# One encoder layer on one core: an earlier scaling, weights in pieces, and a down projection begun with A12

## The chip, the cores and the metric

The kernel runs on one core of a Trainium2 chip. The metric is device time in microseconds: how long one execution takes. A core has five engines that run side by side, each through its own list of instructions in order: TensorE (PE: matmuls and transposes; PEld is its weight load), VectorE (DVE), ScalarE (ACT), GpSimd (POOL) and SyncE (SP, which here issues nearly all DMAs). An instruction that has to wait holds back everything behind it on its engine.

## The reference

The layer is computed for 1024 sample rows and 256 prompt rows, 1024 wide, all in fp32:

```python
h = rmsnorm(x, g_mix);  z = h @ w_in                      # 1024 x 5120
o_a = banded attention, 8 heads with sinks, 2 kv heads    # window 128
o_b = mixture of three dilated groups of 4 heads, weighted by softmax of their log-sums
merged = sigmoid(gate_a) * (o_a @ w_branch_a) + sigmoid(gate_b) * (o_b @ w_branch_b)
x = x + merged @ w_out
h = rmsnorm(x, g_mlp)
x = x + square(relu(h @ w_up)) @ w_down                   # 4096 wide inside
y = rmsnorm(x, g_final)
```

Prompt and sample are two separate sequences with the same weights.

## The kernel before

**Products.** Every fp32 operand is split into a rounded part `hi` (on ACT) and the rest `lo` (on DVE), and a product is three matmuls (hi hi, hi lo, lo hi). For the sample's rows the large products use Strassen's scheme with Winograd's seven products: operands are cut into 2 x 2 blocks, and seven products of sums of blocks (`A11, A12, S2, S3, S1, A22, S4`) give the four blocks of the result. `seven()` is one such product, twelve matmuls with 512 columns; `six()` on L347 holds its matmul, so most matmuls of the profile have that line. The prompt's rows are multiplied plainly by `prompt()`.

**Stages, by the time of the profile.** (1) 0 to 120 us: rows are loaded, normed (`square`: ACT's sum of squares and root; `scale`: DVE's reciprocal and scaling), transposed on PE (`turn`) and split; meanwhile `values` makes the value columns of `z`. (2) 120 to 541 us: the other columns of `z` in pairs of 128 (`pair`, 16 of them); in the last seven, the mixed stage (`late` is true there), the dilated attention is interleaved step by step (`tick`, `beside`). (3) up to about 690 us the banded attention, then gates, merge and output product; this part is ordered by a planner, all others by hand in program order. (4) 890 to 1294 us: the up product in 16 rounds (`up(j)`), whose results `u`, one tile for each of the seven left operands of the next product, are stored in DRAM (`scr_u`). (5) 1294 us to the end: the down product (`Down`).

**Right operands.** `right_pair` is a generator. It loads two tiles of 128 columns (`raw`), forms the sums of blocks `ta`, `tb` and splits four tiles (`raw[0]`, `ta`, `tb`, `raw[1]`); each `yield` is a place where the caller goes on with its own work, and `next` or `steps_of(gen, n)` takes one or n steps. In `pair` the tiles for the next pair are prepared during the present one. The split of a tile is `split_steps`: ACT on L312, DVE on L314; in `Down` and elsewhere `split`: ACT L185, DVE L186.

**Buffers.** Tiles come from pools by kind, and a tile's first writer waits until the buffer is free: `slot` (33 buffers of 4 KB per partition), `wslot` (10 buffers), `stage` (one buffer per name during `up`), the pool `l4` during `Down`. The 28 + 4 buffers of split left operands fill nearly all of `slot` through `up` and come free as the last round ends with each.

**The up rounds.** `up(j)` computes its seven products, the two prompt products, the squared relu of each block and four sums on POOL (L1945 to L1948), then SP stores seven tiles of u. `hooks` is a generator whose steps are taken between products; in the last round it is `Down.begin`, which prepares the first jobs of down. `relu2_sum` (DVE L1873, L1874) finishes a block; `c1`, `c2`, `c7` are ACT's copies of a bank that PE goes on adding to.

**The down product.** `JOBS` is the order of 28 jobs (n, g): n is one of the seven products, g one of four groups of 1024 inner rows. A job is five row tiles t of twelve matmuls. Two neighbouring jobs (g even, g odd) add up in the same five PSUM banks; after the odd one DVE adds each bank to the running sums `v` (L1852) that began as the residual rows from `scr_x`. While job s runs, `ahead(s)` emits the loads and POOL's block differences (`combine`, L1698) for job s + 2 and the splits of the right and left sides for job s + 1: its first step after t = 0, the three left splits after t = 1 to 3. In the last two products of the last groups, and for two more, ACT squares each finished tile for the final norm (`square`, L1806), and POOL multiplies it with the final gain (L1809).

Of the kernel before, what the change touches and what calls it, by code (L numbers as in the profile page):

```python
# [15 lines left out]
P = 128  # L16
# [81 lines left out]
def encoder_kernel(  # L98
# [271 lines left out]
    def right_pair(cols, out, make=wslot, vector=False):  # L370

        raw = [make("raw", (P, KC, P)) for _ in range(2)]
        for i in range(2):
            nc.sync.dma_start(raw[i], cols[i])
        yield

        def part(src, shape):  # L380
            out.append((wslot("whi", shape, F32R), wslot("wlo", shape, F32R)))
            yield from split_steps(*out[-1], src)

        b11, b21, b12, b22 = raw[0][:, :4], raw[0][:, 4:], raw[1][:, :4], raw[1][:, 4:]
        if vector:
# [283 lines left out]
    with ExitStack() as pre:  # L669
# [174 lines left out]
        next(turns[0], None)  # L844
        pss = [bank("mm", "v") for _ in range(2)]
# [5 lines left out]
        square(3)  # L851
        next(turns[1], None)
        scale(3)
# [54 lines left out]
    if True:  # L908
# [104 lines left out]
        def pair(b, parts, cols, nxt, hooks, beside, late):  # L1013
# [6 lines left out]
            nb = right_pair([w_in3[:, :, c : c + P] for c in nxt], np_, wslot, late) if nxt else iter(())  # L1020
# [6 lines left out]
            def behind():  # L1027
                beside()
                if not late:
                    steps_of(b, 2)  # L1030

# [12 lines left out]
            one.direct(NS, NP, pa)  # L1044
            beside()
            seven(x, S2, parts[1], 0, False, False, beside)
# [3 lines left out]
            if late:  # L1050
                next(nb, None)
            z = bank("mm", "z")
            seven(z, S3, parts[1], 1, last=False, mid=beside)
# [3 lines left out]
            beside()  # L1057
            next(hooks, None)
            seven(x, S1, parts[2], 0, False, False, beside)
            two.sum(512, 512, x, c7)  # L1060
            beside()
            if not late:
                steps_of(nb, 3)
# [593 lines left out]
    JOBS = [(n, 2 * p + i) for p in range(NG // 2) for n in range(7) for i in range(2)]  # L1657

    class Down:
        def __init__(self):  # L1660
            self.blocks, self.sums, self.raw, self.rights, self.lefts = {}, {}, {}, {}, {}
            self.t, self.tags, self.late, self.banks, self.rs = {}, 0, None, {}, {}
# [4 lines left out]
        def block(self, g, k, h, make=wslot, queue=None):  # L1667

            b = self.blocks[g, k, h] = [make("raw", (P, 2, 512)) for _ in range(2)]
            for i in range(2):  # L1670
                j = 4 * g + 2 * i
                (queue or nc.sync).dma_start(b[i], w_down4[:, j : j + 2, k, 512 * h : 512 * h + 512])

        def loads(self, n, g):
            if n == 1:
                self.block(g, 1, 1, slot)
            elif n == 4:
                self.block(g, 1, 0, slot)
            elif n == 5 and g < NG - 2:
                self.block(g + 2, 0, 0)  # L1680
                self.block(g + 2, 0, 1)
# [71 lines left out]
        def begin(self):  # L1753

            self.block(0, 0, 0, wslot, nc.scalar)
            self.block(0, 0, 1, slot, nc.scalar)
            self.fetch(*JOBS[0])
            yield
            self.combine(*JOBS[0])
            yield  # L1760
            yield
            self.block(1, 0, 0)
            self.block(1, 0, 1)
            yield
            self.right(*JOBS[0], slot)
            self.combine(*JOBS[1])
# [3 lines left out]
            yield  # L1770
            self.fetch(*JOBS[1])
# [3 lines left out]
        def ahead(self, s):  # L1775
# [6 lines left out]
            if s in (0, 2, 4):  # L1782
                self.residual((C22, C11, C21)[s // 2])
            if s == 0:
                self.residual(C12)
# [42 lines left out]
        def go(self):  # L1828
            with tc.tile_pool(name="down", bufs=1) as self.late:
                for s, (n, g) in enumerate(JOBS):  # L1830
# [6 lines left out]
                    for t in range(5):  # L1837
# [3 lines left out]
                        next(side, None)  # L1841
                        if g % 2 == 0:
                            continue
# [9 lines left out]
                        if g == NG - 1 and n in (3, 4):  # L1853
                            self.square((C22, C12)[n - 3], t)
# [7 lines left out]
    with ExitStack() as pre:  # L1862
# [23 lines left out]
        begun = {}  # L1886

        def up(j, b, parts, hooks):
# [7 lines left out]
            u = [stage(f"u{i}", TH) for i in range(7)]  # L1896
            u11, u12, u22, u21 = u[A11], u[A12], u[A22], u[S3]
# [6 lines left out]
            next(hooks, None)  # L1904
            x, y, c1 = begun[j] if j in begun else next(start)
# [43 lines left out]
            for i in (A11, S1, A22, S2, S3, A12, S4):  # L1949
                nc.sync.dma_start(scr_u[j // 4][:, i, j % 4, :], u[i])  # L1950
# [49 lines left out]
```

## Time and profile before

| | us |
|---|---|
| median of 3 runs | 1686.62 |
| lowest, highest | 1685.78, 1687.19 |
| the profiled execution | 1685.92 |
| its span | 1684.1 |
| PE, PEld busy in it | 1667.8, 1413.9 |
| DVE, ACT, POOL busy in it | 952.2, 718.3, 511.6 |

The granted clock of TensorE was 0.999. Lines of the profile name an engine, a line of the kernel (L347), what is written and read (`dn<-dhi,ulo`), and times in us. In the lists in order of time the first number is the start from the span's beginning, the second the length; x2 stands for two instructions in one row; in brackets stands the engine's idle time just before and what ended it. SPq is SP's queue of DMA issues: its length is the time that SP took to issue, waits included, and not the transfer. Matmuls are pipelined, so the next one starts before the one before ends.

### The profile page before, as it was taken

To read this page: it belongs to the slowest core of one execution; us is meant where nothing else is said; L and a number is where in the kernel's file an instruction comes from. 1 tells how busy PE (TensorE), PEld (TensorE's weight loads), DVE (VectorE), ACT (ScalarE), POOL (GpSimd) and SP (SyncE) were. 2 spreads that over 40 slices of the span, in tenths; PEclk is the share of its full clock that TensorE was granted. 3 is DMA by queue.
4 is the path that set the end of the run, shared out by engine and by line. 5 is a ranking of instruction groups with operands and counts; after the bars stand their busy time and mean duration, and the time that the engine had idled before them with its cause. 6 is when DMAs were issued, how large, how long until landed. Compare 5 with 4: busy or idle time off the path is not lost.

```text
span 1684.1 us, 24915 instructions
## 1 busy us (share of the span) xinstructions
PE 1667.8 (99%) x9268; PEld 1413.9 (84%) x9268; DVE 952.2 (57%) x1544; ACT 718.3 (43%) x1485; POOL 511.6 (30%) x404
## 2 busy tenths in 40 slices
PE   8999999999999999999999999999999999999998
PEld 7898888887788888888888888888888888888886
DVE  6732233455563565677278445545457767666575
ACT  6332323346663556654175333333334333333345
POOL 1312222122111463200100646556456322314150
PEclk9999999999999999999999999999999999999999
DMA  7416552677676793845121443443346845533333
GB/s 247 150 58 127 134 129 77 163 193 196 191 198 189 202 244 118 293 130 198 38 88 58 160 152 111 136 160 119 121 160 241 293 155 166 207 101 114 119 119 125
DMA packets 224408, 260.35 MB, mean 155 GB/s; under 512 B 29568, under 2 KB 154288, under 8 KB 224288
## 3 DMA queue, kind: packets, MB, share of 16 engines
q1 hardware_dynamic: 214976, 235.60, 44.1%
q0 software_dynamic: 7936, 20.54, 5.5%
q10 hardware_dynamic: 1376, 2.62, 0.4%
q8 instruction: 73, 1.20, 0.3%
q14 instruction: 47, 0.39, 0.1%
HBM read 173.03 MB, written 90.92 MB: 157 GB/s over the span
## 4 chain that ended last, share of the span: by engine, by line
PE 92%; DVE 3%; ACT 2%; DMA 1%; issue 1%; SPq 1%; POOL 0%; DVEq 0%; ACTq 0%
PE dn L347 20%; PE x L347 19%; PE mm L192 14%; PE z L347 9%; PE v L794 5%; PE mm L347 5%; PE y L347 5%; PE sc L347 3%; PE pv L347 3%; PE pv L1173 1%; PE pt L1157 1%; PE sc L537 1%; PE pv L582 1%; PE pt L569 1%; PE sc L1131 1%
## 5 line engine op out<-in xcount | busy, mean ns | idle before, releaser
L347 PE MATMUL dn<-dhi,ulo 128*128 128x512 f32 x448 | 174.5, 390 | 2.0 <-DVE ulo L186 2.0
L347 PE MATMUL dn<-dlo,uhi 128*128 128x512 f32 x448 | 174.3, 389 | 0.0
L347 PE MATMUL dn<-dhi,uhi 128*128 128x512 f32 x448 | 174.3, 389 | 0.0
L347 PE MATMUL x<-chi,wlo 128*128 128x512 f32 x424 | 167.2, 394 | 1.7 <-DVE wlo L314 1.6
L347 PE MATMUL x<-clo,whi 128*128 128x512 f32 x424 | 165.7, 391 | 0.1
L347 PE MATMUL x<-chi,whi 128*128 128x512 f32 x424 | 165.1, 389 | 0.0
L314 DVE TENSOR_TENSOR wlo<-ta,whi 128x1024 fp32r<-128x1024 f32 x30 | 55.7, 1857 | 178.5 <-ACT whi L312 178.5
L314 DVE TENSOR_TENSOR wlo<-raw,whi 128x1024 fp32r<-128x1024 f32 x60 | 90.4, 1506 | 97.8 <-ACT whi L312 97.8
L389 POOL TENSOR_TENSOR tb<-raw 128x512 f32<-128x512 f32 x25 | 32.8, 1312 | 364.4 <-DMA raw<-in_w_in_dram 147.0
L347 PEld LDWEIGHTS dn<-dhi,ulo 128*128 128x128 f32 x448 | 84.1, 188 | 20.3 <-DVE ulo L186 2.8
L186 DVE TENSOR_TENSOR ulo<-uraw,uhi 128x1024 fp32r<-128x1024 f32 x56 | 92.4, 1669 | 11.6 <-ACT uhi L185 11.6
L347 PEld LDWEIGHTS dn<-dhi,uhi 128*128 128x128 f32 x448 | 84.1, 188 | 17.4
L347 PEld LDWEIGHTS dn<-dlo,uhi 128*128 128x128 f32 x448 | 84.1, 188 | 17.3
L347 PEld LDWEIGHTS x<-chi,wlo 128*128 128x128 f32 x424 | 79.8, 188 | 17.8 <-DVE wlo L314 1.3
L347 PEld LDWEIGHTS x<-chi,whi 128*128 128x128 f32 x424 | 79.6, 188 | 17.0
L347 PEld LDWEIGHTS x<-clo,whi 128*128 128x128 f32 x424 | 79.8, 188 | 14.8 <-DVE clo L314 0.4
L1698 POOL TENSOR_TENSOR t<-raw,t 128x1024 f32<-128x1024 f32 x16 | 46.6, 2928 | 144.0 <-DMA raw<-in_w_down_dram 144.0
L1852 DVE TENSOR_TENSOR v<-v,dn 128x512 f32<-128x512 f32 x90 | 59.5, 681 | 39.7 <-PE dn L347 35.5
L1945 POOL TENSOR_TENSOR u<-u,u 128x640 f32<-128x640 f32 x16 | 25.6, 1597 | 159.3 <-ACT u L1870 159.3
L347 PE MATMUL dn<-dhi,up 128*128 128x512 f32 x224 | 73.5, 389 | 0.0
L347 PE MATMUL z<-chi,wlo 128*128 128x512 f32 x184 | 72.0, 391 | 0.0
L347 PE MATMUL z<-chi,whi 128*128 128x512 f32 x184 | 71.6, 389 | 0.0
(325 smaller groups left out, 4619.9 us busy)
## 6 DMA issues: line engine op xcount, KB each, us to landing
scr_u<-u SPq DMA_DIRECT2D x112, 320.0 KB, 2.6
uraw<-scr_u SPq DMA_DIRECT2D x56, 512.0 KB, 4.5
raw<-in_w_in_dram SPq DMA_DIRECT2D x33, 512.0 KB, 5.7
raw<-in_w_up_dram SPq DMA_DIRECT2D x32, 512.0 KB, 5.4
raw<-in_w_down_dram SPq DMA_DIRECT2D x28, 512.0 KB, 6.8
sg<-scr_g SPq DMA_DIRECT2D x32, 256.0 KB, 6.4
uraw<-scr_u SPq DMA_DIRECT2D x28, 256.0 KB, 4.5
v<-scr_v SPq DMA_DIRECT2D x96, 64.0 KB, 2.7
```

Of the source, the lines that this page charges most:

```text
L186: nc.vector.tensor_tensor(lo, src, hi.bitcast(F32), op=ALU.subtract)
L192: nc.tensor.matmul(ps, a, b, start=i == 0, stop=i == len(seq) - 1)
L314: nc.vector.tensor_tensor(lo, src, hi.bitcast(F32), op=ALU.subtract)
L347: nc.tensor.matmul(ps, a, b, start=first and i == 0, stop=last and i == len(seq) - 1, skip_group_check=True)
L389: (nc.vector if vector else nc.gpsimd).tensor_tensor(o, x, y, op=ALU.subtract)
L537: nc.tensor.matmul(at(k, h)[p0 : p0 + nq, :], qk[rows, p0 : p0 + nq], qk[rows, P + P * a : P + P * a + W], start=True, stop=True, skip_gro ...
L569: nc.tensor.transpose(ps[:, P * a : P * a + P], s[:, h, P * k : P * k + P], ident)
L582: nc.tensor.matmul(pv[HALVES[h], c + p0 : c + p0 + nq], v[:, a + k, HALVES[h]], pt[:, 2 * k + h, p0 : p0 + nq], start=k == 0, stop=k == W ...
L794: nc.tensor.matmul(ps[:, :n], a, b, start=k == 0 and j == 0, stop=k == KC - 1 and j == 2)
L1698: nc.gpsimd.tensor_tensor(o, a, b, op=ALU.subtract)
L1852: nc.vector.tensor_tensor(v, v, ps, op=ALU.add)
L1945: nc.gpsimd.tensor_tensor(u[S1], u21, u22, op=ALU.add)
```

## The change

Seven things are edited; the number of matmuls stays the same.

- At the start, `square(3)` and `scale(3)` are emitted before the first values products, not after them.
- In the mixed stage the two loads of a pair's weights become eight pieces, one for each step, and the steps begin after the prompt product, one product earlier.
- In the first up round two steps of the next round's right side are taken between the two prompt products.
- u's stores are emitted in the next round, after its first products (and once at the end).
- The first pair of groups in `JOBS` begins with n = 6, whose left side is A12 and whose right side is a block of the weights as it is; `Down.begin`, the loads and the residual's order follow from it. A block that n = 6 needs is loaded two rounds before the end of up into a place of its own; since n = 5 needs it again, it is loaded again at n = 4, where the next groups' blocks are now loaded too.
- `Down.begin` no longer issues DMAs on ACT.
- The squares of n = 3 and 4 in the last group are kept in a list and emitted after the next tile's products and splits.

```diff
+    def right_pair(cols, out, make=wslot, vector=False, step=KC):
         raw = [make("raw", (P, KC, P)) for _ in range(2)]
         for i in range(2):
-            nc.sync.dma_start(raw[i], cols[i])
-        yield
+            for c in range(0, KC, step):
+                nc.sync.dma_start(raw[i][:, c : c + step, :], cols[i][:, c : c + step, :])
+                if step < KC:
+                    yield
+        if step == KC:
+            yield
...
         scale(2)
         next(turns[0], None)
+        square(3)
+        scale(3)
         pss = [bank("mm", "v") for _ in range(2)]
...
         next(turns[2])
-        square(3)
         next(turns[1], None)
-        scale(3)
         square(4)
...
+            nb = right_pair([w_in3[:, :, c : c + P] for c in nxt], np_, wslot, late, 2 if late else KC) if nxt else iter(())
+            def piece():
+                if late:
+                    next(nb, None)
+            def piece_beside():
+                beside()
+                piece()
...
             one.direct(NS, NP, pa)
+            piece()
             beside()
-            seven(x, S2, parts[1], 0, False, False, beside)
+            seven(x, S2, parts[1], 0, False, False, piece_beside)
...
             behind()
-            if late:
-                next(nb, None)
+            piece()
             z = bank("mm", "z")
-            seven(z, S3, parts[1], 1, last=False, mid=beside)
+            seven(z, S3, parts[1], 1, last=False, mid=piece_beside)
...
             beside()
+            piece()
             next(hooks, None)
-            seven(x, S1, parts[2], 0, False, False, beside)
+            seven(x, S1, parts[2], 0, False, False, piece_beside)
             two.sum(512, 512, x, c7)
             beside()
-            if not late:
+            if late:
+                steps_of(nb, 2)
+            else:
                 steps_of(nb, 3)
...
-    JOBS = [(n, 2 * p + i) for p in range(NG // 2) for n in range(7) for i in range(2)]
+    JOBS = [(n, 2 * p + i) for p in range(NG // 2) for n in (range(7) if p else (6, *range(6))) for i in range(2)]
...
         def loads(self, n, g):
-            if n == 1:
+            if n == 6 and g == 0:
+                self.block(1, 0, 0)
+                self.block(1, 0, 1)
+            elif n == 1:
                 self.block(g, 1, 1, slot)
             elif n == 4:
                 self.block(g, 1, 0, slot)
-            elif n == 5 and g < NG - 2:
-                self.block(g + 2, 0, 0)
-                self.block(g + 2, 0, 1)
+                if g < NG - 2:
+                    self.block(g + 2, 0, 0)
+                    self.block(g + 2, 0, 1)
...
         def begin(self):
-            self.block(0, 0, 0, wslot, nc.scalar)
-            self.block(0, 0, 1, slot, nc.scalar)
             self.fetch(*JOBS[0])
             yield
-            self.combine(*JOBS[0])
-            yield
-            yield
-            self.block(1, 0, 0)
-            self.block(1, 0, 1)
+            self.block(1, 1, 0)
             yield
             self.right(*JOBS[0], slot)
-            self.combine(*JOBS[1])
+            yield
+            self.fetch(*JOBS[1])
             yield
             self.left(*JOBS[0], 0)
             self.left(*JOBS[0], 1)
-            yield
-            self.fetch(*JOBS[1])
+            self.block(0, 0, 0)
+            self.block(0, 0, 1)
             yield
             self.left(*JOBS[0], 2)
...
-            if s in (0, 2, 4):
-                self.residual((C22, C11, C21)[s // 2])
-            if s == 0:
-                self.residual(C12)
+            if s < 4:
+                self.residual((C11, C22, C12, C21)[s])
...
                         next(side, None)
+                        if self.pending:
+                            self.square(*self.pending.pop())
                         if g % 2 == 0:
                             continue
...
                         if g == NG - 1 and n in (3, 4):
-                            self.square((C22, C12)[n - 3], t)
+                            self.pending.append(((C22, C12)[n - 3], t))
...
+        stores_u = []
+        def store_u():
+            while stores_u:
+                nc.sync.dma_start(*stores_u.pop(0))
...
             next(hooks, None)
+            store_u()
+            u = [stage(f"u{i}", TH) for i in range(7)]
+            u11, u12, u22, u21 = u[A11], u[A12], u[A22], u[S3]
             x, y, c1 = begun[j] if j in begun else next(start)
...
                 steps_of(nb, 4)
                 prompt_out(prompt(parts[0]), (u11, u21))
+                steps_of(nb, 2)
             prompt_out(prompt(parts[3], "sc"), (u12, u22))
...
-            for i in (A11, S1, A22, S2, S3, A12, S4):
-                nc.sync.dma_start(scr_u[j // 4][:, i, j % 4, :], u[i])
+            stores_u.extend((scr_u[j // 4][:, i, j % 4, :], u[i]) for i in (A11, S1, A22, S2, S3, A12, S4))
...
         for j in range(last + 1):
+            if j == last - 1:
+                down.block(0, 1, 0, lambda name, shape: late.tile(list(shape), F32, name=name, tag="block", bufs=2))
             b = up(j, *b, entering() if not j else down.begin() if j == last else iter(()))
+        store_u()
```

More of the change, by code (lines that the diff above doesn't have):

```diff
@@ L368, in prompt @@
         return ps
-    def right_pair(cols, out, make=wslot, vector=False):
+    def right_pair(cols, out, make=wslot, vector=False, step=KC):
         raw = [make("raw", (P, KC, P)) for _ in range(2)]
         for i in range(2):
-            nc.sync.dma_start(raw[i], cols[i])
-        yield
+            for c in range(0, KC, step):
[4 more added lines that the diff above has]
+            yield
         def part(src, shape):
@@ L1019, in pair @@
             np_ = []
-            nb = right_pair([w_in3[:, :, c : c + P] for c in nxt], np_, wslot, late) if nxt else iter(())
+            nb = right_pair([w_in3[:, :, c : c + P] for c in nxt], np_, wslot, late, 2 if late else KC) if nxt else iter(())
             def halfway(gen=None):
@@ L1661, in __init__, with block @@
             self.blocks, self.sums, self.raw, self.rights, self.lefts = {}, {}, {}, {}, {}
-            self.t, self.tags, self.late, self.banks, self.rs = {}, 0, None, {}, {}
+            self.t, self.tags, self.late, self.banks, self.rs, self.pending = {}, 0, None, {}, {}, []
         def make(self, name, shape=(P, 2, 512), dt=F32):
             return self.late.tile(list(shape), dt, name=name, tag="l4", bufs=8)
-        def block(self, g, k, h, make=wslot, queue=None):
+        def block(self, g, k, h, make=wslot):
             b = self.blocks[g, k, h] = [make("raw", (P, 2, 512)) for _ in range(2)]
@@ L1671, in block @@
                 j = 4 * g + 2 * i
-                (queue or nc.sync).dma_start(b[i], w_down4[:, j : j + 2, k, 512 * h : 512 * h + 512])
+                nc.sync.dma_start(b[i], w_down4[:, j : j + 2, k, 512 * h : 512 * h + 512])
         def loads(self, n, g):
-            if n == 1:
+            if n == 6 and g == 0:
+                self.block(1, 0, 0)
+                self.block(1, 0, 1)
+            elif n == 1:
                 self.block(g, 1, 1, slot)
@@ L1894, in prompt_out @@
                     relu2(d[:, 512:], ps[:, P * i : P * i + P])
-            u = [stage(f"u{i}", TH) for i in range(7)]
-            u11, u12, u22, u21 = u[A11], u[A12], u[A22], u[S3]
             start = begin(parts)
```

## The prediction

> **What bounds the kernel now.** I read the page's first part, then who TensorE waited for, then the instructions around each of those waits in order of time, and last the rows of the engines that released them.
>
> ```profile
> PE 1667.8 (99%) x9268; PEld 1413.9 (84%) x9268; DVE 952.2 (57%) x1544; ACT 718.3 (43%) x1485; POOL 511.6 (30%) x404
> ```
>
> TensorE (PE) is busy 99% of the span, and the change neither adds nor removes a matmul. So only places where PE stands still can give time, and any new standstill costs it one for one. This is what PE waited for, longest first:
>
> ```profile
> core 0 of [0], span 1684.1 us
> engine line waited for: us in total, times, longest us
> PE dn L347 <- DVE ulo L186: 2.0, 2, 1.2
> PE tr L338 <- DVE xn L739: 1.6, 2, 0.9
> PE x L347 <- DVE wlo L314: 1.6, 2, 1.1
> ```
>
> The first and third rows are two waits each; with the one at 26.21 below they are five, and each stands at a place that the diff edits. In order of time (start, length, engine, line, and in brackets the idle time before):
>
> ```profile
> 26.21 0.30 PE L338 MATMUL tr<-ident,xn 128*128 128x128 f32 x1 [1.10 <-DVE tab L856]
> ...
> 928.90 0.50 PE L347 MATMUL x<-chi,wlo 128*128 128x512 f32 x1 [1.08 <-DVE wlo L314]
> ...
> 935.15 0.47 PE L347 MATMUL x<-chi,wlo 128*128 128x512 f32 x1 [0.49 <-DVE wlo L314]
> ...
> 1295.23 0.39 PE L347 MATMUL dn<-dhi,uhi 128*128 128x512 f32 x1
> 1296.85 0.50 PE L347 MATMUL dn<-dhi,ulo 128*128 128x512 f32 x1 [1.23 <-DVE ulo L186]
> ...
> 1609.33 0.50 PE L347 MATMUL dn<-dhi,ulo 128*128 128x512 f32 x1 [0.75 <-DVE ulo L186]
> ```
>
> The brackets count from the modelled end of the matmul before (1295.23 + 0.39 to 1296.85 is 1.23), but matmuls overlap. In the chain of work twelve of this shape take
>
> ```profile
> 1280.48 2.72 PE z L347 x12
> ```
>
> so one goes out every 0.23 us, and each wait costs 0.39 - 0.23 = 0.16 us more than its bracket: 1.26, 1.24, 0.65, 1.39 and 0.91 us, together 5.45.
>
> **The change part by part.** The sum is made against the profiled execution, 1685.92 us (1684.1 span and 1.8 around it); the median of the runs is 0.7 above it, 1686.62.
>
> *Early scaling.* `square(3)` and `scale(3)` go ahead of the values' products in the order of ACT and DVE. Engine by engine, ACT first:
>
> ```profile
> 21.98 1.21 ACT L765 ACTIVATE hhi<-tr 128x256 fp32r<-128x256 f32 x4 [4.30 <-PE tr L338]
> 23.05 1.08 ACT L732 ACTIVATE xn<-xt 128x1024 f32<-128x1024 f32 x1
> ...
> 24.78 1.28 DVE L739 SCALAR_TENSOR_TENSOR xn<-xt,rs,gm 128x1024 f32<-128x1024 f32 x1
> ```
>
> ACT stood idle 4.30 us before 21.98, so the 1.08 us of tile 3's square fit there, and its scaling on DVE, 1.28 us, ends well ahead of 24.78. What was behind the square, ACT's copies of tile 1 out of PSUM, then ends about 1.3 us earlier as well, and PE reaches tile 3's transposes at 26.21 - 1.26 = 24.95. I take all of 1.26 off. Ends: 0 (if the wait was for the table's memset on L856) and 1.26. Next late could be the sample rows and value weights that SP loads; nothing of theirs makes PE wait before 120 us.
>
> *Weights in pieces.* These are the DMAs by their tiles, with KB each and median us from issue to landing:
>
> ```profile
> uraw<-scr_u SPq DMA_DIRECT2D x56, 512.0 KB, 4.5
> raw<-in_w_in_dram SPq DMA_DIRECT2D x33, 512.0 KB, 5.7
> ...
> raw<-in_w_down_dram SPq DMA_DIRECT2D x28, 512.0 KB, 6.8
> ...
> v<-scr_x SPq DMA_DIRECT2D x20, 256.0 KB, 5.6
> qk<-scr_kb SPq DMA_DIRECT2D x36, 128.0 KB, 3.2
> ```
>
> In the mixed stage (`late`) each of six loads of two `raw` of 512 KB becomes eight DMAs of 128 KB, one per step, begun one product earlier. SP issues 36 more DMAs. The issues beside, q, k and v tiles of the attention, are no longer behind 1 MB. None of that stage's lines (L537, L569, L582) is in the rows of PE's waits above, so I take 0; the ends are in the rivals.
>
> *Split between the prompt products.* Two more steps (ACT `whi<-ta`, DVE `wlo<-ta`) are emitted in `up(0)` between the two prompt products. DVE's rows, then ACT's:
>
> ```profile
> 927.10 1.75 DVE L314 TENSOR_TENSOR wlo<-ta,whi 128x1024 fp32r<-128x1024 f32 x1 [4.76 <-ACT whi L312]
> 931.83 0.69 DVE L1873 TENSOR_TENSOR u<-y,c 128x512 f32<-128x512 f32 x1 [2.98 <-POOL u L1947]
> ```
>
> ```profile
> 924.99 0.28 ACT L1869 ACTIVATE u<-sc 128x128 f32<-128x128 f32 x1 [1.75 <-PE sc L347]
> ```
>
> DVE was idle 4.76 us before 927.10 and ACT 1.75 us before 924.99: the split of `ta` fits into these and ends near 925.6, ahead of PE, which is there at 928.90 - 1.24 = 927.66. The split of `tb` moves up by one place too, out from behind L1873, which waits for POOL until 931.83: ready just ahead of 935.15 before, it now is before 929. Both waits go: 1.24 + 0.65 = 1.89. Next late is ACT's `c7`, which PE needs for A22 at 927.66 + 3 x 2.72 = 935.8 and which stands behind two `relu2` that wait for a store of u; I estimate 0.6 us of room, so 0 lost; ends 0 and 1.89 gained.
>
> *Stores of u.* They are emitted in the next `up`; on SP nothing but the last `up`'s fetch of A12 passes them: 0. The extra 1 MB of `block(0, 1, 0)` goes out two `up`s before, where nothing waits behind it: 0. The second load of that block for n = 5 adds 1 MB for g = 0 and 1, at n = 4, behind the part that is wanted first: 0.
>
> *Down begun with A12.* Its right side is raw weight, so POOL's subtractions before the first job go, and ACT's four DMA issues with them. POOL's rows, before:
>
> ```profile
> 1292.64 6.40 POOL L1698 TENSOR_TENSOR t<-raw 128x1024 f32<-128x1024 f32 x2 [4.46 <-DMA raw<-in_w_down_dram]
> 1299.01 2.02 POOL L1945 TENSOR_TENSOR u<-u,u 128x640 f32<-128x640 f32 x1
> ```
>
> Without these 6.40 us, and with the splits emitted one to two products earlier, I estimate DVE done with the first job's `ulo` and `up` by 1292.5. PE is through with the prompt product at 1296.85 - 1.39 - 6 x 0.23 = 1294.1 and goes straight on: 1.39 off, ends 0 and 1.39. Two `dhi`, about 1 us each, now are ahead of `c7` on ACT; PE wants it 2 x 2.72 us after 1280.48, at 1285.9, and I estimate it for 1285.5: 0, with little room, and at most 0.5 lost.
>
> What comes late next is the third job, (0, 0). Its DMAs stand behind the last store of u, which waits for POOL's four sums. They took from 1299.01 until SP's fetch went out at 1309.00; now they can begin at about 1295.5, 1.4 us behind the prompt product, and the fetch follows at about 1305.3. The fetch is the same (two `uraw` of 512 KB and one of half), but now `block(1, 0, 0)` and `block(1, 0, 1)` (4 x 512 KB) go ahead of the first residual row (`v`, 256 KB):
>
> ```profile
> 1309.00 0.94 SPq L1718 DMA_DIRECT2D uraw<-scr_u  x2
> ```
>
> ```profile
> 1316.00 0.69 DVE L1852 TENSOR_TENSOR v<-v,dn 128x512 f32<-128x512 f32 x1 [1.45 <-DMA v<-scr_x]
> ```
>
> ```profile
> 1302.00:1312.00 10.00, 10.00 (x46) 8.28 (x45) 8.24 (x5) 2.60 (x3) 6.56 (x3) 1.00 0.66 233
> 1312.00:1322.00 10.00, 10.00 (x46) 8.29 (x45) 5.63 (x7) 5.62 (x7) 0.00 (x0) 1.00 1.02 370
> ```
>
> (the windows' last numbers are GB/s). From issue to the first row it took 7.0 us, of which 1.57 MB at 370 GB/s are 4.2; 2.1 MB more are 5.7; from 1305.3 that makes 1318.0. DVE's add of job 2 waits for it, and behind the add, on DVE, are the splits of job 3's left sides. POOL's subtraction for job 4 runs just then, and the two hold each other up, as these rows of POOL and DVE show:
>
> ```profile
> 1601.45 6.75 POOL L1698 TENSOR_TENSOR t<-raw,t 128x1024 f32<-128x1024 f32 x2
> ```
>
> ```profile
> 1605.86 4.55 DVE L186 TENSOR_TENSOR ulo<-uraw,uhi 128x1024 fp32r<-128x1024 f32 x2
> ```
>
> (the first of the two `ulo` could end only at 1609.28, after POOL's second at 1608.20). So: add to 1318.7, `ulo` to 1321.8, add, `ulo` to 1323.7. Two jobs of 60 matmuls are 27.2 us, so PE begins job 3 at 1321.3, and wants the second `ulo` six matmuls later, at 1322.7. I take 1.05 us lost; ends 0 (sums of u done 2 us sooner) and 7 (below).
>
> *Squares one tile behind.* In n = 3, g = 3 ACT's square waits for the add and holds back the split that DVE's next step needs, so both engines go in lockstep. With the square behind the split DVE is some 4 us earlier in n = 4, so `ulo` at 1609.28 is ready before 1608.4: 0.91 off; ends 0 (POOL alone held it) and 0.91. The kernel's end is untouched.
>
> Sum: -1.26 - 1.89 - 1.39 + 1.05 - 0.91 = -4.4. Profiled 1681.5; with the 0.7 the median is 1682.2.
>
> **The rivals.**
>
> *Given back in the third job or the squares don't help.* If POOL alone set 1609.33, 0.91 stays; if the third job loses 2 to 3 us instead of 1.05, the rest goes: 1683.2 to 1686. For it: DVE's splits had nothing to spare there before either. Against: POOL's subtraction at 1601.45 can itself begin earlier once ACT's squares don't hold POOL's products back. 0.25.
>
> *Slower: residual rows far too late.* Same place, one mechanism: whatever the first row is later than 1318.0 PE loses whole. It decides from 1322.4 on, which asks for 256 GB/s instead of 370 over the 3.67 MB (14.3 us after 2.8 of start); the window before shows 233, though SP was waiting with its issues there. At 233 the row lands 6 us later: 5.45 - 7 is a loss of 1.6, 1688; with the next rows as late again, 1691. 0.09.
>
> *Slower: pieces too small.* If the eight pieces of 128 KB went one after another, they would take 8 x 3.2 = 25.6 us, and DVE's subtractions want the last, by the products and the attention's work between them, some 25 us after the first is issued. Each 0.2 us more per piece would then hold DVE 1.6 us, in six loads up to 9.6 us: 1692. Against: they need not follow one another, since SP issues the next without waiting. 0.06. The Trainium skill, in "DMA: Bandwidth & Descriptors", section "Bandwidth", says to batch DMAs to 1 MiB or more for three quarters of the peak rate; by that rule the kernel would end at this rival's 1692 instead of 1682.2. The trace agrees that a quarter of the bytes takes more than a quarter of the time, 3.2 against 6.8 us.
>
> *The change doesn't do what it says* at the start, if the transposes waited for the memset on L856 and that stays where it is: 1.26 stays, 1683.4. It is within the first rival's chance.
>
> **How the numbers follow.** Forecast 0.60 (1680.9 to 1683.2: from nothing given back, 1686.62 - 5.45 less some noise, to a gain of 3.4), given back 0.25, the two slower ones 0.15. A measurement of this kernel tells about 0.2% from no change, 3.4 us. The forecast is faster, most of the second case is within, the last two slower: 0.61, 0.25, 0.14. The range leaves out part of the slower cases: 1680.7 to 1688.0.
>
> **What would show it.** The five rows of PE's waits gone; a wait of about 1 us on `ulo` 27 us after PE enters down; no new wait on L537. Wrong would make it: a wait on A22 for `c`, an attention tile landing late in the mixed stage, a later residual row than computed, or another order in the part that a planner orders (690 to 885 us), of which this trace can show nothing.

## The result, and the profile after

| | before | after |
|---|---|---|
| median, us | 1686.62 | 1680.89 |
| lowest, highest | 1685.61, 1688.09 | 1679.83, 1681.33 |
| profiled execution, its span | 1685.92, 1684.1 | 1681.33, 1679.5 |

The ratio is 0.9962, with a 95% interval of 0.9951 to 0.9974: 5.7 us faster by the medians of five runs each, 6.4 us by the ratio (1686.62 x 0.0038), where 4.4 was forecast. Run again twice, the changed kernel stood at 1681.44 (ratio 0.9966, 0.9954 to 0.9978) and 1681.26 (0.9964, 0.9951 to 0.9976), 5.2 and 5.7 us below the kernel before beside it. By 0.9962 the time is 1680.2, half a microsecond under the forecast's range, which began at 1680.7. The interval reaches from 1678.4 to 1682.2, so the forecast of 1682.2 lies at its very end; it is the traces below that show the size to be short. The direction held, and so did the mechanisms of the four waits; the size did not.

The first part of the page of the changed kernel, and whom TensorE waited for:

```profile
PE 1667.2 (99%) x9268; PEld 1414.5 (84%) x9268; DVE 951.4 (57%) x1544; ACT 718.2 (43%) x1485; POOL 512.1 (30%) x404
```

```profile
engine line waited for: us in total, times, longest us
PE warm L711 <- POOL ident masks.py:199: 1.4, 1, 1.4
PE tr L338 <- DVE xn L743: 1.2, 2, 0.9
PE sc L1146 <- DVE m L1148: 1.0, 2, 0.7
PE v L798 <- DVE vlo L705: 0.7, 1, 0.7
PE sc L541 <- DMA qk<-scr_kb: 0.5, 1, 0.5
PE mm L192 <- ACT z L999: 0.2, 1, 0.2
```

PE does the same work, and the rows `dn <- ulo`, `x <- wlo` and the wait for `tab` are gone: all five waits. Of what is left, POOL's `ident` and DVE's `xn`, `m` and `vlo` were there before; two rows are new, 0.5 us on the keys of the mixed stage (`qk<-scr_kb`) and 0.2 us on `z`; and one more is gone, 0.3 us of `PE pt L1157 <- ACT s L1143`, of which more below. The loss at the third job of down is in none of these rows; it is smaller than a bracket shows. In order of time, the places of the five waits, with the third job (1318.53 on) ahead of the last:

```profile
25.05 1.04 PE L338 MATMUL tr<-ident,xn 128*128 128x128 f32 x8
...
926.74 0.40 PE L347 MATMUL x<-chi,wlo 128*128 128x512 f32 x1
926.97 0.40 PE L347 MATMUL x<-clo,whi 128*128 128x512 f32 x1
...
932.20 0.39 PE L347 MATMUL x<-chi,wlo 128*128 128x512 f32 x1
...
1292.38 0.39 PE L347 MATMUL dn<-dhi,ulo 128*128 128x512 f32 x1
...
1318.53 0.47 PE L347 MATMUL dn<-dhi,ulo 128*128 128x512 f32 x1
1318.84 0.40 PE L347 MATMUL dn<-dlo,uhi 128*128 128x512 f32 x1
...
1320.22 0.50 PE L347 MATMUL dn<-dhi,ulo 128*128 128x512 f32 x1
1320.56 0.40 PE L347 MATMUL dn<-dlo,uhi 128*128 128x512 f32 x1
...
1604.59 0.39 PE L347 MATMUL dn<-dhi,ulo 128*128 128x512 f32 x1
```

Where PE still waits a little, the matmul is longer: 0.47 and 0.50 us at 1318.53 and 1320.22, and the next goes out 0.31 and 0.34 us behind it, not 0.23 as elsewhere (926.74 to 926.97). The rows of the kernel before that the prediction quoted have the same 0.50 and 0.47 at each matmul of 512 columns that had to wait.

All kernels here run 9268 PE instructions that agree in shape and in the names of their tiles from the first to the last (where the order of the products changed, in the first half of down, each place has another product of the same shape), so their starts can be compared one by one. What each trace gains (-) or loses against the first trace of the kernel before, in us, by the stretch in which it does, worked out from the starts:

```
                 start    near   rest of   up     begin   third  near
                 26       614    30-921    930    of down  job   1605
before, again      0.00   +0.01   +2.71   +0.01   -0.03    0.00   -0.01
after             -1.29   -0.76   +1.04   -2.15   -1.53   +0.77   -1.04
after, again      -1.29   -0.76   +1.30   -2.15   -1.53   +0.56   -1.04
after, third      -1.29   -0.76   +1.19   -2.15   -1.53   +0.55   -1.04
e1 scale late     +0.01   -0.65   +0.89   -2.15   -1.53   +0.35   -1.04
e2 whole          -1.29   +0.08   +2.35   -2.15   -1.53   +0.65   -1.04
e3 no split       -1.29   -0.76    0.00   +0.01   -1.53   +0.73   -1.04
e4 down as was    -1.29   -0.73   +1.87   -2.15   +0.40   +0.02   -1.04
e5 squares now    -1.29   -0.76   +2.62   -2.15   -1.53   +0.57   +0.02
e6 rows first     -1.29   -0.76   +2.70   -2.15   -1.53    0.00   -1.04
e6 again          -1.29   -0.76   +1.43   -2.15   -1.53    0.00   -1.04
e8 bias on SP     -1.29   -0.75   +2.56   -2.15   -1.53    0.00   -1.04
e10 rows later    -1.29   -0.74   -0.15   -2.15   -1.53   +1.73   -1.04
```

Four columns (26, 930, the begin of down, 1605) are fixed to a few hundredths: each part gives its gain in every trace that has it and in no other. So is the one near 614, to about a tenth: 0.65 to 0.76 us are gone in all eleven traces with weights in pieces and in none of the three with whole weights. The prediction had no gain there. The third column, the rest of the mixed stage and of what follows it up to 921 us, is for the most part chance: from -0.15 to +2.71, for kernels that are alike there too. The trace that the prediction read has nearly the least of it.

### The profile page after: what moved, and what is told of

The parts are those of the page before. It is cut to its first block, busy times and chain, and to the rows that moved or that the text cites. A ratio compares the mean times of both kernels' runs of the same rounds, so it can differ in the third digit from the quotient of the medians.

```text
span 1679.5 us, 24942 instructions
## 1 busy us (share of the span) xinstructions
PE 1667.2 (99%) x9268; PEld 1414.5 (84%) x9268; DVE 951.4 (57%) x1544; ACT 718.2 (43%) x1485; POOL 512.1 (30%) x404
## 5 line engine op out<-in xcount | busy, mean ns | idle before, releaser
L186 DVE TENSOR_TENSOR ulo<-uraw,uhi 128x1024 fp32r<-128x1024 f32 x56 | 88.7, 1606 | 3.5 <-ACT uhi L185 3.5
L186 DVE TENSOR_TENSOR dlo<-raw,dhi 128x1024 fp32r<-128x1024 f32 x32 | 48.6, 1540 | 47.2 <-ACT dhi L185 46.3
L185 ACT ACTIVATE dhi<-raw 128x1024 fp32r<-128x1024 f32 x32 | 33.5, 1058 | 93.5 <-PE dn L347 93.0
```

The costliest lines, as they stand in the source:

```text
L185: nc.scalar.activation(hi, src, AF.Copy)
L186: nc.vector.tensor_tensor(lo, src, hi.bitcast(F32), op=ALU.subtract)
```

## The experiments

Times are medians; the kernel before was between 1686.59 and 1687.04 beside them. Every kernel computes the whole layer.

### The changed kernel and the kernel before once more

Neither has an edit.

> The changed kernel once more, to settle its size. By the waits that its profile shows (the instructions of TensorE, matched one by one with those of the kernel before, end 4.9 us sooner: 1.25 + 2.0 + 1.5 + 1.0 gained, 0.7 given back at the third job of down, 0.1 in the mixed stage) the medians should differ by 4.6 to 4.9 us, near 1681.8. If something that those waits do not show had gone as well, the difference would stay at the 5.7 us of its first runs, near 1680.9.

> The kernel before once more, for a second profile. Five waits that the change was made against are there in full (1.25, 1.24, 0.65, 1.39 and 0.91 us, within 0.05 each) if they are fixed in the program; one that is not there again, or comes in another size, was chance in the first profile. Between 370 and 720 us the trace may differ from the first by up to 2 us, as the traces of the changed kernel's variants differ among themselves there: they wait there for loads and row maxima now here, now there.

> The changed kernel, beside the next two on the same chip. If the fixed waits alone make the difference to the kernel before (1.29 + 2.15 + 1.53 + 1.04 less 0.6 at the third job of down, and 0.2 in the mixed stage: 5.6), the medians differ by 5.2 to 5.7 us; by 4.9 or less if the first profile's sum of gains and chance losses is the whole of it. The loss at the third job is there again, between 0.35 and 0.8 us.

The changed kernel took 1681.44 and 1681.26, so 5.2 and 5.7 us less than the kernel before beside it: the first lies between the two sizes expected for it (4.6 to 4.9, and 5.7), the second at the upper end of the 5.2 to 5.7 that the fixed waits alone would make. The kernel before was the same as itself (1686.74, ratio 0.9997, 0.9987 to 1.0007). These rows are from its second profile, first whom PE waited for, then single waits:

```profile
PE dn L347 <- DVE ulo L186: 1.9, 2, 1.2
PE x L347 <- DVE wlo L314: 1.6, 2, 1.1
...
PE tr L338 <- DVE tab L856: 1.1, 1, 1.1
...
PE mm L192 <- ACT z L995: 0.8, 1, 0.8
...
PE pt L1157 <- ACT s L1143: 0.5, 2, 0.3
PE sc L537 <- DMA qk<-scr_kb: 0.4, 2, 0.2
```

```profile
26.28 0.95 PE L338 MATMUL tr<-ident,xn 128*128 128x128 f32 x7 [1.10 <-DVE tab L856]
...
1299.62 0.50 PE L347 MATMUL dn<-dhi,ulo 128*128 128x512 f32 x1 [1.20 <-DVE ulo L186]
...
1612.09 0.50 PE L347 MATMUL dn<-dhi,ulo 128*128 128x512 f32 x1 [0.74 <-DVE ulo L186]
```

The five waits are there again within 0.03 us. What differs lies before 921 us, where this trace lost 2.7 us. Rows that the first one did not have (`z`, the keys, a second wait for `s`) are 1.4 us of it by their brackets, which leave out part of each wait. So the wait on the keys is not new with the change: the kernel before has it as well, in some executions. In two more traces of the changed kernel it is absent; the same window, 370 to 720 us, of the first of them:

```profile
PE sc L1146 <- DVE m L1148: 0.7, 1, 0.7
PE pt L1172 <- ACT s L1158: 0.3, 1, 0.3
PE mm L192 <- ACT z L999: 0.2, 1, 0.2
```

### Each gain undone by itself

```diff
-        square(3)          # e1: back behind the products of the values
-        scale(3)
         pss = [bank("mm", "v") for _ in range(2)]
...
                 prompt_out(prompt(parts[0]), (u11, u21))
-                steps_of(nb, 2)                     # e3
             prompt_out(prompt(parts[3], "sc"), (u12, u22))
...
-                            self.pending.append(((C22, C12)[n - 3], t))   # e5
+                            self.square((C22, C12)[n - 3], t)
```

> Squares and scaling of the fourth row tile go back behind the products of the values, all else as changed. Theory: the wait of 1.25 us near 26 us comes back alone: 1.25 us slower than the changed kernel, span near 1680.7. Rival: the rows of the first stage are late anyway and a part of it is waited for elsewhere: under 0.6 us. For the wait of 0.5 us on the keys at 451 us: if pieces of weights cause it, it stays; if it is only that TensorE comes 1.2 us earlier, it is gone here, and the net loss is 0.7 us.

> The two steps of the split between the prompt products of the first up group are left to the place where the kernel before had them. Theory: both waits, 1.24 us near 928 us and 0.65 us near 934 us, come back: 2.0 us slower than the changed kernel, span near 1681.5. Rival: one wait follows from the other, and only the first, 1.3 us, comes back.

> The squares of down's last sums are taken at once again, all else as changed. Theory: POOL's scaling behind each square holds VectorE near the end, and the wait of 0.9 us near 1604 us comes back: 1.0 us slower than the changed kernel, span near 1680.5. Rival: the wait came from the order in which the jobs stood before and does not come back: within 0.2 us.

They took 1682.17, 1683.29 and 1681.84 (ratios to the kernel before 0.9976, 0.9981 and 0.9971), 0.4 to 2.4 us more than the changed kernel took in its own three runs (1680.89 to 1681.44), none of them beside these. One row of each, of whom PE waited for, in the order e1, e3, e5:

```profile
PE tr L338 <- DVE tab L860: 1.1, 1, 1.1
```

```profile
PE x L347 <- DVE wlo L314: 1.6, 2, 1.1
```

```profile
PE dn L347 <- DVE ulo L186: 0.7, 1, 0.7
```

Each wait is back alone and whole: 1.30, 2.16 and 1.06 us in the table. That is what the theories said, and their rivals, by which only part of a wait or none of it would come back, fall. For the wait on the keys e1 had a second question, whether PE's earlier arrival makes it; it is gone in e1, but also in the changed kernel's other two traces, so that proves nothing.

How the squares do it shows on DVE and POOL. First the changed kernel, then e5, in each DVE's rows and then POOL's:

```profile
1595.27 3.41 DVE L186 TENSOR_TENSOR dlo<-raw,dhi 128x1024 fp32r<-128x1024 f32 x1
1598.61 3.44 DVE L186 TENSOR_TENSOR ulo<-uraw,uhi 128x1024 fp32r<-128x1024 f32 x2
...
1591.85 5.75 POOL L1716 TENSOR_TENSOR t<-raw,t 128x1024 f32<-128x1024 f32 x2
```

```profile
1598.60 4.89 DVE L186 TENSOR_TENSOR dlo<-raw,dhi 128x1024 fp32r<-128x1024 f32 x2 [1.74 <-ACT dhi L185]
1603.41 4.55 DVE L186 TENSOR_TENSOR ulo<-uraw,uhi 128x1024 fp32r<-128x1024 f32 x2
...
1599.00 6.74 POOL L1716 TENSOR_TENSOR t<-raw,t 128x1024 f32<-128x1024 f32 x2
```

e5's PE is 1.4 us behind up to there. Beyond that `ulo` begins 3.4 us later in it and POOL's subtraction 5.8 us later, so that the two meet (1599.00 to 1605.74, and `ulo` from 1603.41). With the squares deferred the subtraction is over at 1597.60, before `ulo` begins.

### Weights whole again

```diff
-            nb = right_pair([...], np_, wslot, late, 2 if late else KC) if nxt else iter(())
+            nb = right_pair([...], np_, wslot, late) if nxt else iter(())
...
             def piece():
-                if late:
-                    next(nb, None)
+                pass
...
             behind()
-            piece()
+            if late:
+                next(nb, None)
             z = bank("mm", "z")
...
-            if late:
-                steps_of(nb, 2)
-            else:
+            if not late:
                 steps_of(nb, 3)
```

> The weights of the mixed stage are loaded whole again, all else as changed. The changed kernel has one new wait in this stage, 0.5 to 0.6 us on the keys' load (qk<-scr_kb) at 451 us. Theory: the pieces of weights stand in the queue ahead of that load and make it late; with whole weights it is gone, and the wait of 0.2 us at 457 us that the kernel before had comes back: 0.4 us sooner than the changed kernel. Rival one: the keys had no slack before either (landed at 451.94, wanted at 452.03) and TensorE merely comes earlier now: the wait of 0.5 us stays. Rival two: pieces of 128 KB move their bytes so badly that whole weights make the stage shorter by more than 1 us.

It took 1682.31, 0.9 us more than the changed kernel beside it (1681.44); the runs of the two overlap (1681.11 to 1683.31, 1680.15 to 1682.95), and the profiled run is the slowest of its seven. The wait on the keys at 451 us is gone, as the theory said; but of the eleven traces with pieces only four have 0.2 us or more of it, and the second one of the kernel before, with whole weights, has 0.2 us as well. So neither the pieces nor PE's earlier arrival is what makes it; it comes and goes, and the theory falls with the first rival. Whether pieces make it likelier these traces can't tell.

Two delays do go with whole weights: they are in all three traces that have them (two of the kernel before and this one) and in none of the eleven with pieces, except for 0.1 us of the second in e1. One is the 0.2 us at 457 us that the theory had come back. The other is 0.75 us at 614 us, in the banded attention. It stood in the first trace of the kernel before; here are PE's row, then DVE's and POOL's just ahead of it, and last DVE's at the same place in the changed kernel's third trace:

```profile
614.51 0.77 PE L1157 MATMUL pt<-ident,s 128*128 128x128 f32 x5 [0.27 <-ACT s L1143]
```

```profile
609.77 1.45 DVE L1137 SCALAR_TENSOR_TENSOR nm_a<-m,nsink 128x2 f32<-128x2 f32 x1
...
612.21 0.85 DVE L1137 SCALAR_TENSOR_TENSOR nm_a<-m,nsink 128x2 f32<-128x2 f32 x1
...
609.65 1.55 POOL L1316 TENSOR_TENSOR merged<-merged,r 128x512 f32<-128x512 f32 x1
```

```profile
608.92 0.16 DVE L1152 SCALAR_TENSOR_TENSOR nm_a<-m,nsink 128x2 f32<-128x2 f32 x1
...
610.43 0.45 DVE L1152 SCALAR_TENSOR_TENSOR nm_a<-m,nsink 128x2 f32<-128x2 f32 x1
```

`nm_a`, two numbers for each partition, takes 1.45 us instead of 0.16 and ends as POOL's sum ends (611.22 and 611.20). ACT's `s` waits for it, and PE for `s`. In the three traces with whole weights the two `nm_a` take 2.3 to 2.4 us together, in the eleven with pieces 0.5 to 1.7. With pieces POOL's sums stand elsewhere against PE, up to 3.5 us apart from trace to trace; with whole weights they stand at one place within 0.1 us. What moves them was not followed up, so another execution with pieces may meet the delay again. Together the two delays are 0.95 us, which is about the 0.9 between the medians.

The prediction's rival of pieces that move too slowly, and the second one here, fall too: whole weights do not make the stage shorter. The Trainium skill, in "DMA: Bandwidth & Descriptors", section "Bandwidth", asks for batches of 1 MiB or more. By that rule the prediction had 1692 for the pieces; the trace of the whole weights, which at 512 KB are below that size too, shows no gain from batches four times as large.

### Down begun as before

```diff
-    JOBS = [(n, 2 * p + i) for p in range(NG // 2) for n in (range(7) if p else (6, *range(6))) for i in range(2)]
+    JOBS = [(n, 2 * p + i) for p in range(NG // 2) for n in range(7) for i in range(2)]
...
         def begin(self):
+            self.block(0, 0, 0, wslot, nc.scalar)
+            self.block(0, 0, 1, slot, nc.scalar)
             self.fetch(*JOBS[0])
...          # loads, residual rows and stores of u likewise in the old order
```

> The down stage begins with S1 as in the kernel before, with its loads, residual rows and stores in the old order; the other parts stay changed. Theory: the wait of 1.4 us at the start of down comes back (1.5 us in the matched instructions), and the 0.66 us given back at the third job is gone: 0.8 us slower than the changed kernel, span near 1680.3. Rival: the third job's loss does not come from the new order (it is POOL's combine, which runs anyway): then the whole 1.5 us come back and the loss at 27 us into down stays, span near 1681.0.

1681.92, 0.5 us more than the changed kernel beside it. The row of whom PE waited for:

```profile
PE dn L347 <- DVE ulo L186: 1.6, 1, 1.6
```

The wait at the start of down is back, 0.4 us longer than in the kernel before (by the table PE is there 2.3 us sooner than in that kernel's first trace, and the two `ulo`, which begin at 1290.38 instead of 1292.24, only 1.9), and the loss at the third job is gone (+0.02). So that loss comes with the new order, and the rival falls. This part's net gain is 1.53 + 0.40 - 0.6 = 1.3 us in PE's time, of which 0.3 do not reach the end: from the end of ACT's last instruction to the end of the span, the time of the last store, it is 3.7 us here and in both traces of the kernel before, and 3.8 to 4.0 us in those with the new order. Why the last store takes longer with the new order was not followed up.

### The residual rows sooner, and later

```diff
         def ahead(self, s):
...
-            self.loads(n, g)
             if s < 4:
                 self.residual((C11, C22, C12, C21)[s])
+            self.loads(n, g)        # e6; e10 instead: residual(C22), residual(C11) at s = 0, none at s = 1
```

> In the first four jobs of down the residual rows are issued ahead of the weights instead of behind them; nothing else moves. Theory: the first row lands some 5.4 us sooner (four loads of 512 KB stand ahead of it now, landing 1.35 us apart), so the sum into it ends before POOL's combine begins at 1312.6 us and the low halves for the third job are in time: the 0.66 us are gone, span near 1678.9. Rival one: the weights, which land 3.4 us later (five rows of 0.68 us), make the combine for the fourth job late, and the same wait comes back one job on: no gain or a loss of up to 1 us. Rival two: the row was not what held the low halves: no change.

> The residual rows ahead of the weights again, for its time. In the matched instructions this took back the whole of the third job's loss (0.35 to 0.8 us over the runs of the changed kernel), so the median should lie 0.4 to 0.7 us under that of the changed kernel beside it; if it is not lower, the later weights cost elsewhere what the rows gain.

> The opposite of the rows first: in the first job of down the five rows of the other block (C22) go ahead of the five that the second job's sums need (C11), so these land 3.4 us later (five of 0.68 us), near 1317.9. If the lateness of the row alone sets the third job's loss, as the prediction's second rival had it, it grows one for one, from 0.6 to 4.0 us. If the loss is made of the late row and POOL's combine together (VectorE's low half takes 3.3 us instead of 1.2 because POOL runs from 1312.6 to 1317.4), the low halves now come behind the combine and take 1.2 us each: the sum into the first row at 1318.0, the low halves done at 1319.8 and 1321.7, TensorE wants them at 1318.2 and 1.4 us later, so the loss is 2.0 us.

With the rows first: 1680.96 and 1680.83 (ratios 0.9963 and 0.9959, the second 0.9946 to 0.9971); with the rows later: 1682.40 (0.9974). DVE's and POOL's rows at the third job in the changed kernel, with the rows first, and with the rows later:

```profile
1314.56 0.69 DVE L1865 TENSOR_TENSOR v<-v,dn 128x512 f32<-128x512 f32 x1 [4.58 <-DMA v<-scr_x]
1315.17 3.27 DVE L186 TENSOR_TENSOR ulo<-uraw,uhi 128x1024 fp32r<-128x1024 f32 x1
1318.35 0.67 DVE L1865 TENSOR_TENSOR v<-v,dn 128x512 f32<-128x512 f32 x1
1318.95 1.21 DVE L186 TENSOR_TENSOR ulo<-uraw,uhi 128x1024 fp32r<-128x1024 f32 x1
...
1312.60 4.76 POOL L1716 TENSOR_TENSOR t<-raw 128x1024 f32<-128x1024 f32 x2 [4.97 <-DMA raw<-in_w_down_dram]
```

```profile
1311.53 0.68 DVE L1865 TENSOR_TENSOR v<-v,dn 128x512 f32<-128x512 f32 x1
1312.13 1.22 DVE L186 TENSOR_TENSOR ulo<-uraw,uhi 128x1024 fp32r<-128x1024 f32 x1
...
1317.55 4.76 POOL L1716 TENSOR_TENSOR t<-raw 128x1024 f32<-128x1024 f32 x2 [8.29 <-DMA raw<-in_w_down_dram]
```

```profile
1316.33 0.69 DVE L1867 TENSOR_TENSOR v<-v,dn 128x512 f32<-128x512 f32 x1 [7.58 <-DMA v<-scr_x]
1316.93 1.22 DVE L186 TENSOR_TENSOR ulo<-uraw,uhi 128x1024 fp32r<-128x1024 f32 x1
1318.07 0.68 DVE L1867 TENSOR_TENSOR v<-v,dn 128x512 f32<-128x512 f32 x1
1318.66 1.22 DVE L186 TENSOR_TENSOR ulo<-uraw,uhi 128x1024 fp32r<-128x1024 f32 x1
...
1310.98 4.75 POOL L1716 TENSOR_TENSOR t<-raw 128x1024 f32<-128x1024 f32 x2 [4.59 <-DMA raw<-in_w_down_dram]
```

In the changed kernel the add waits 4.58 us for its row, and the `ulo` behind it takes 3.27 us instead of 1.22: POOL's subtraction runs from 1312.60 to 1317.36, and `ulo` ends 1.08 us behind it, so that it can hardly have begun before. With the rows first the add does not wait, `ulo` is done at 1313.35, before POOL begins, and the third job loses nothing; the weights that now come later make no new wait, so rivals one and two fall. (The profile here, at 1682.18, was the slowest of that run's five; before 921 us it has 2.7 us of chance waits in the table, the second trace 1.4.)

With the rows later they land 3.4 us later in their queue; the sum into the first is 1.8 us later by the clock and, since this trace's PE is 1.2 us ahead there by the table, 2.9 us later against PE. The loss is 1.73 us, 1.1 more than the mean of 0.6, not the 2.9 or 3.4 more of one for one: `ulo` begins after POOL's end at 1315.73 and is short again. So the loss was made by two things together, the late row and POOL's subtraction, and the meeting alone costs `ulo` 2 us. The Trainium skill, in "SBUF — State Buffer", section "Who interferes with whom", says that a DVE instruction with two inputs in SBUF contends with a GpSimd instruction that reads SBUF, over a shared pair of ports that is an exclusive lock; the three lengths here, 3.27, 1.22 and 1.22, agree.

With the rows first the medians are 0.5 and 0.4 us below the changed kernel's beside them. The runs' spread (1.6 to 2.8 us) does not settle that, but both traces show the 0.35 to 0.8 us gone.

### Biases through SP's queue

```diff
-        nc.gpsimd.dma_start(b, toeplitz(g + 1, 2 * P, -64, 2 * i))
+        nc.sync.dma_start(b, toeplitz(g + 1, 2 * P, -64, 2 * i))
...          # likewise the other three gathers of load_bias_b; on top of the rows first
```

> The kernel with the rows first, and the biases of the mixed stage's attention gathered through SP's queue behind the keys instead of POOL's beside them. Theory: the keys are late by chance (0.5 us at 451, 1.5 us at 424, 1.0 us at 477 in three traces) because a gather of biases that POOL issued 1.3 to 2 us before or after them is moved at the same time; in one queue behind them it no longer can, and no wait on keys is left between 370 and 480 us: 0.3 to 1 us under the kernel with the rows first, and less spread between runs. Rival: SP's queue is the tighter one there, and the gathers make the next values and keys late: slower by 1 us or more.

It took 1682.97, 2.1 us more than the rows first alone beside it (no run of the one is as fast as any of the other), and its profile still has the wait:

```profile
PE sc L541 <- DMA qk<-scr_kb: 0.6, 1, 0.6
```

The theory that a gather beside them makes the keys late falls, at least as the only cause. The kernel is slower by what the rival said, 1 us or more; that SP's queue makes values and keys late is not shown, since the profiled run is the fastest of the eight and its rest up to 921 us (+2.56) is no larger than that of the rows first alone (+2.70). What sets the chance waits between 370 and 720 us stays open; the runs show only that they are there in both kernels, at a handful of places, and change from execution to execution.

## Why four mechanisms were right, one gain was not foreseen, and the size was short

*Early scaling*: right. 1.26 was the price, 1.29 the gain, and the rival that the memset sets the wait falls with e1.

*Weights in pieces*: taken at 0, since none of that stage's lines was among PE's waits; 0.95 us gained, 0.2 at 457 us and 0.75 at 614 us, and no cost seen. That gain is luck by the prediction's own account: it has no mechanism for it, and the larger part lies behind the stage, where POOL's sums met DVE. The line to be watched (L537, now L541) did wait 0.5 us in the first trace, by chance. In the rival of the small pieces the 6.8 us set against the keys' 3.2 are those of down's weights; the loads that were cut took 5.7.

*Split between the prompt products*: both waits gone, as said; 2.15 measured for 1.89. `c7` was in time: no such wait is in the rows.

*Down begun with A12*: no wait stands where PE waited for `ulo` (1292.38), nor at A22 for `c`; 1.53 for 1.39, before the third job and the end.

*Squares*: 1.04 for 0.91, and DVE's lead about as said (3.4 us for some 4), and POOL's subtraction out of `ulo`'s way, as its rival's counterargument had it.

*The third job*: the chain that the prediction laid out (fetch behind the last store, two blocks ahead of the first row, the add, `ulo` held by POOL's subtraction) is what the trace has. Its size was wrong: 1.05 taken, 0.35 to 0.77 lost, 0.6 in the mean of seven traces. Counted from PE's start of the job, every step of the chain from the fetch on came 0.3 to 0.5 us sooner than worked out: the prediction had PE without a wait at 1321.3 and the row at 1318.0, 3.3 us ahead; the trace has PE's start without a wait at 1318.22 (1318.53 less 0.31) and the row at 1314.5, 3.7 us ahead. Its second rival, that "PE loses whole" whatever the row is later, is refuted by the rows put later: 2.9 us more of lateness cost 1.1.

**The steps that failed** are three terms of the sum and the range's low end. First and largest, "I take 0" for the weights in pieces: 0.95 were gained. The reason given looked at the mixed stage's lines alone; the row `PE pt L1157 <- ACT s L1143: 0.3` of the same list, at a place behind that stage, was not priced; by the matched starts it cost 0.75 us. Second, "each wait costs 0.39 - 0.23 = 0.16 us more than its bracket": a wait of a 512-column matmul also costs the next one about 0.10, since that goes out 0.34 us behind it and not 0.23; the 0.50 stood in the rows quoted. Over the four parts that is 0.03 + 0.26 + 0.14 + 0.13 = 0.56 us. Third, the 1.05 given back, 0.45 too much. With the three, less the 0.3 at the end, 4.4 becomes 6.1; the three comparisons gave 5.7, 5.2 and 5.7 by the medians and 6.4, 5.7 and 6.1 by the ratios. Last, the low end of 1680.7 was 1.5 us under the forecast, "from nothing given back ... less some noise". It allowed for one term, while the chance waits before 921 us alone set these traces up to 2.9 us apart (-0.15 to +2.71), which moves a median of five too.

## What to carry to other kernels

Compare two traces of the same kernel before pricing a gain of a few microseconds: waits that return to the hundredth are the program's, and those that come and go are the width of the forecast. Price a wait of TensorE from start to start, and include the next start too, not only the idle time. Where a result of DVE is the last thing before a matmul, look at what POOL runs just then: at 614 us, at the third job and at the squares, a few microseconds between the two decided over 0.4 to 1 us of PE's time, and one of the three had shown only as a wait on ACT.

## What the runs showed of the hardware that was not expected

- A matmul of 512 columns that PE had waited for was 0.50 us long, not 0.39, and its successor went out 0.34 us behind it, not 0.23. A short delay shows in this way only: at 1318.53 there is no bracket, and 0.3 us are lost.
- The same program on the same data differed by up to 2.7 us in one stretch (30 to 921 us), while the places of the five waits agreed to 0.03 us.
- A load that came 2.9 us later against PE cost 1.1 us, because the work behind it no longer met POOL: `ulo` 1.22 us instead of 3.27. A DVE instruction on two numbers per partition took 1.45 us instead of 0.16 in such a meeting.
